# Joining the split of six gated forms, dividing one step of the last down stage, and holding an evacuation behind two weights

## The chip, the cores and the metric

The kernel runs on one core of a Trainium2 chip. The metric is device time in microseconds (us). TensorE is PE in the profile, its weight loads PEld, VectorE is DVE, ScalarE is ACT, GpSimd is POOL, and SP is the engine that issues most of the transfers.

## What is computed

One layer of an encoder on 512 tokens of width 1024: a mixer (a gated short convolution beside a forgetting attention, merged by two sigmoid gates, and an output projection), then a channel mixer, then a norm. The change lies in the channel mixer:

```
h = rms_norm(x, norm_ffn_g[l])
up = causal_dwconv(h @ w_up[l], conv_ffn_w[l])      # 1024 -> 2 * 2816, three taps in time
a, b = jnp.split(up, 2, axis=-1)
x = x + (jax.nn.silu(a) * b) @ w_down[l]            # 2816 -> 1024
```

All data are float32.

## The kernel before, in words

**Numbers in two parts.** Every matmul operand is split: hi is a rounded copy made by ACT (fp32r), lo is the rest, a subtraction on DVE. A product then costs three matmuls: hi·hi, lo·hi, hi·lo. For weights this split is `split()` (L253): ACT's copy at L275 gives `wh_...`, DVE's subtraction at L279 gives `wl_...`. Both have two buffers in turn, so a chunk's split can start when the chunk two places before it is through with PE.

**The stream.** Weights come as a list of chunks (L125 to L154), used in this order by `chunk()` (L290). `split()` also issues loads (L182, on SP) up to seven chunks ahead, as far as raw buffers are free: four for up and P chunks together, four for F chunks.

**The channel mixer.** The 2816 hidden columns are 22 blocks j of 128. `PHASES` (L43) cuts them into j = 0 to 11 and 12 to 21. Each phase has an up stage (one `up(j, ph)` per block, L1141) and then a down stage (`seven(STEPS[ph], ...)`, L824). For each j, `up` makes two products of 48 matmuls (the a half with i = 0, the b half with i = 1) and evacuates each: `mul` on DVE (L1171, times the norm), three taps (`taps`, L564: a scaled copy on ACT at L566, two DVE additions at L567 and L570); after the second, `glu` (L1227) runs the silu on ACT (L1231) and multiplies. In the very last j it also runs a small Sqrt (L1233), so that ACT's table is loaded in time for the last norm. Blocks j of `SUP` are computed by `seven` instead.

**Seven products.** The down products use a seven-product scheme for 2×2 blocks. A pair q holds j = 2q and 2q + 1 (each in two halves of 256 tokens); its seven forms are two blocks of data as they are, and sums. `ge` is the even j, `go` holds the odd j in two pieces and the four sums t1 to t4 (`t13`, L1252, and `t24`, L1256, both on DVE): six forms of 256 columns. `hl` (L1260) splits forms into `gh` (ACT, L1262) and `gl` (DVE, L1263). A step of `STEPS` multiplies one or two (i, q): i is a pair of output blocks. A step is two chunks: P (three products per pair, raw weights) and F (four products, sums of weights that DMAs build in DRAM ahead of time: `make_forms`, L190, with puts on SP at L208 and adds on POOL at L211, a group of up to two steps of the same size). A double step has 18 matmuls in P and 24 in F, a single one 9 and 12. `passes` (L315) runs the hi weights against hi and lo data first, form by form, then the lo weights. P wants the first, second and seventh form of a pair, in that order. In the stream P18/F18 to P29/F29 are the steps of phase 0; P30 to P33 are `SUP` blocks; P34/F34 to P41/F41 are the steps of phase 1.

**Who orders the work.** PE's matmuls and the DMAs are pinned in program order. On ACT, DVE and POOL the framework places an operation when it takes it to be ready, earlier ones of the program first, unless it is told otherwise. The kernel tells it through a list `later` of (first chunk k, cost in us, tags, function). Each `split()` ends with `run_later(k, us)` (L224), which takes from the list what is due and fits an allowance: 1.7 at an up chunk, 1.6 at P, 0.75 at F (4.2, 1.6 and 1.2 while evacuations tagged `e` are waiting in the list). The first due item that doesn't fit ends it. What it runs stands in `after_split()` (L159), so it queues behind the last split's hi on ACT and lo on DVE. `seven` splits one chunk ahead (`split_next`, L818) and calls `flush(wants[name])` (L843), which forces what a P or F chunk needs. `glu` for an odd j first forces the forms of all earlier pairs (L1238), then appends its own, due at chunk k plus 2, 3, 4, or, for the last j of a phase, plus 4, 5, 6; k is the last chunk split so far. In the last j of a phase the multiplication into `go` is itself appended, due at k + 3, on DVE; in others POOL does it at once (L1243).

**The seam.** When the last `up` of a phase has issued its second product, it calls `split_next()` (the first P chunk) and, only if evacuations tagged `e` wait, also flushes them and splits the first F chunk (L1162 to L1166). By then in both phases none wait, so the last evacuation follows P's split at once, and the F chunk is split by `seven`, after P's matmuls in the program.

Of the kernel before, what the change touches and what calls it, by code (L numbers as in the profile page):

```python
# [42 lines left out]
PHASES = ((0, 12), (12, NP))  # L43
# [4 lines left out]
STEPS = (  # L48
    tuple(((i, q), (i, q + 1)) for i, q in ((0, 0), (0, 2), (1, 0), (1, 2), (0, 4), (1, 4)))
    + tuple(((i, q), (i, q + 1)) for i in (3, 2) for q in (0, 2, 4)),  # L50
    (((2, 6), (2, 7)), ((2, 8), (2, 9)), ((0, 6), (0, 7)), ((0, 8), (2, 10)), ((0, 9), (0, 10)))
    + (((1, 6),), ((1, 7), (1, 8)), ((1, 9), (1, 10))),
)

# [16 lines left out]
def block_kernel(ctx, tc, xT, vecs, wv, win, wmix, wo, wup, wst, wdp, outT):  # L71
# [10 lines left out]
    def keep(ins):  # L82
        return tc.keep_in_program_order(ins)
# [72 lines left out]
    later = []  # L156
    held = dict.fromkeys(NRAW, 0)

    def after_split():  # L159

        st = ExitStack()
        for ins in order.values():
            st.enter_context(tc.issue_after(ins))
        return st

    def tag_of(k):
        return "raw" if stream[k][0][0] != "F" else "rf" if k >= ff0 else "rg"

    def load(upto):
        for k in range(len(raws), min(upto, len(stream) - 1) + 1):  # L170
            nm, src, ncol = stream[k]
            tag = tag_of(k)
            if held[tag] == NRAW[tag] or tag not in pools:
                return
            held[tag] += 1
            raw = pools[tag].tile([P, D], F32, tag=tag, name=f"raw_{nm}", bufs=NRAW[tag])
            if k == 0:

                keep(nc.scalar.dma_start(raw[:, VB:ncol], src[:, VB:]))
                keep(nc.sync.dma_start(raw[:, :VB], src[:, :VB]))  # L180
            else:
                keep(nc.sync.dma_start(raw[:, :ncol], src if tag == "raw" else made[src]))  # L182
            raws.append(raw[:, :ncol])
# [34 lines left out]
    def slot():  # L218

        while todo_bg and todo_bg[0][0] <= make_forms.slot:  # L220
            todo_bg.pop(0)[1]()
        make_forms.slot += 1

    def run_later(k, us):  # L224

        n = 0
        while n < len(later):
            if later[n][0] <= k and later[n][1] <= us + 0.1:
                us -= later[n][1]
                with after_split():  # L230
                    later.pop(n)[3]()
            elif later[n][0] <= k:
                return
            else:
                n += 1
# [11 lines left out]
    def flush_only(tags):  # L247

        while n := [n for n, w in enumerate(later) if set(w[2]) & set(tags)]:
            with after_split():  # L250
                later.pop(n[0])[3]()

    def split(hl=None):  # L253

        k = len(parts)
        if k == len(stream):
            return
        nm, _, ncol = stream[k]
        load(k + (LOOK if len(raws) > KB else AHEAD))
        if hl is None:  # L260
            hl = []
            for x in "hl":
                if k == 0:
                    wp.tile([P, PADW[x]], F32, tag=f"pad{x}", name=f"pad_{x}")
                w0 = VOFF if k < KB else 0
                hl.append(wp.tile([P, D], F32R, tag=f"w{x}", name=f"w{x}_{nm}", bufs=2)[:, w0 : w0 + ncol])
        hi, lo = hl
        raw = raws[k]
        if k == 0:
            for cs in (slice(VB, S + H), slice(0, VB)):  # L270
                keep(nc.vector.tensor_copy(hi[:, cs], raw[:, cs]))
        elif k == 1:
            keep(nc.vector.tensor_copy(hi, raw))
        else:
            ins = nc.scalar.activation(hi, raw, AF.Copy)  # L275
            order["hi"] = ins.ins
            if k < KB:
                keep(ins)
        ins = nc.vector.tensor_sub(lo, raw, hi.bitcast(F32))  # L279
        order["lo"] = ins.ins  # L280
        if k < KB:
            keep(ins)
        held[tag_of(k)] -= 1
        parts.append((hi, lo))
        if any(("e",) in w[2] for w in later):
            run_later(k, {"u": 4.2, "P": 1.6, "F": 1.2}[nm[0]])
            return
        run_later(k, {"u": 1.7, "P": 1.6, "F": 0.75, "i": 3.0, "m": 3.0, "d": 0 if nm == "dp1" else 2.1}.get(nm[0], 3.5))
# [163 lines left out]
    for kb in range(KB):  # L452
        x = xs[kb]
# [236 lines left out]
    z, e, o = (ap.tile([n, S], F32, tag="pp", name=nm, bufs=NPP) for nm in ("fz", "fe", "fo"))  # L690
# [83 lines left out]
    for q in (0, 2):  # L774
        f, g = x_sums(slice(q, q + 2))
# [8 lines left out]
    for idx in late:  # L784
        kind, i = divmod(idx, 4)
# [9 lines left out]
    for i in range(n + LA):  # L795
# [8 lines left out]
        if 0 <= i - LA < n:  # L804
            pr, e, qb = units[i - LA]
# [335 lines left out]
    def up(j, ph, rb2, pu=None):  # L1141
        uu = []

        def tap(i, z):
            u = fp.tile([P, S], F32, tag="fu", name=f"fu{j}{i}", bufs=3)
            taps(u, z, CF + 3 * (2 * j + i))
            uu.append(u)

        if j in SUP[ph]:
            c = 2 * SUP[ph].index(j)  # L1150
            slot()
            seven(
                UPD[ph][c : c + 2], NU[ph] + c, {j: USETS[j]}, lambda q, g: up_form(ph, q, g), of="x",
                done=lambda i, banks, ids: merge(ph, j, banks, ids, rb2, tap, uu),
            )
            slot()
            return
        evacs = []
        for i in range(2):
            slot()  # L1160
            p = pu[i] if pu else block(f"up{2 * j + i}", x1h, x1l, True)
            if i and j + 1 == PHASES[ph][1]:  # L1162
                split_next()
                if any(("e",) in w[2] for w in later):
                    flush_only((("e",),))
                    split()  # L1166
            z = [None]

            def mul(i=i, p=p, z=z):
                z[0] = fp.tile([P, S], F32, tag="fz", name=f"fz{j}{i}", bufs=4)  # L1170
                nc.vector.tensor_mul(z[0], p, rb2)  # L1171

            evac = [(0.7, mul), (1.4, lambda i=i, z=z: tap(i, z[0]))]
            if i:
                evac.append((0, lambda: glu(ph, j, uu)))
            if any(("e",) in w[2] for w in later):
                later.extend((0, us, (("e",), acc.last) if x == 0 else (("e",),), f) for x, (us, f) in enumerate(evac))
            else:
                for _, f in evac:
                    f()  # L1180
# [46 lines left out]
    def glu(ph, j, uu):  # L1227
        a, b = uu
        q, k = j // 2, len(parts) - 1
        g0 = place(ph, q)  # L1230
        nc.scalar.activation(a, a, AF.Silu)  # L1231
        if j == NP - 1:
            nc.scalar.activation(tbl, a[: 4 * H, :1], AF.Sqrt, scale=0.0, bias=eps[: 4 * H])  # L1233
        if j % 2 == 0:
            ge = glu.even = fp.tile([P, 2, 2 * P], F32, tag="ge", name=f"ge{q}", bufs=2)
            keep(nc.gpsimd.tensor_mul(ge, a.rearrange(halves_of, h=2), b.rearrange(halves_of, h=2)))  # L1236
            return
        flush_only([("q", x) for x in range(q)])  # L1238
        ge = glu.even
        go = fp.tile([P, 6, 2 * P], F32, tag="gr", name=f"go{q}")  # L1240

        def mul(eng):
            return eng.tensor_mul(go[:, 0:2, :], a.rearrange(halves_of, h=2), b.rearrange(halves_of, h=2))  # L1243

        if j + 1 < PHASES[ph][1]:
            keep(mul(nc.gpsimd))
        else:
            later.append((k + 3, 0.7, (("q", q),), lambda: mul(nc.vector)))
        b11, b12 = ge[:, 0, :], ge[:, 1, :]
        b21, b22, t1, t2, t3, t4 = (go[:, i, :] for i in range(6))  # L1250

        def t13():  # L1252
            nc.vector.tensor_sub(t1, b11, b12)
            nc.vector.tensor_sub(t3, b22, b12)

        def t24():  # L1256
            nc.vector.scalar_tensor_tensor(t2, t1, -1.0, b22, op0=ALU.mult, op1=ALU.subtract)
            nc.vector.scalar_tensor_tensor(t4, t2, -1.0, b21, op0=ALU.mult, op1=ALU.subtract)

        def hl(src, gs):  # L1260
            def f():
                nc.scalar.activation(gh[:, gs, :], src, AF.Copy)  # L1262
                nc.vector.tensor_sub(gl[:, gs, :], src, gh.bitcast(F32)[:, gs, :])  # L1263

            return f


        d = (2, 3, 4) if j + 1 < PHASES[ph][1] else (4, 5, 6)
        w = [(d[0], 0.85, t13), (d[0], 0.85, t24), (d[1], 0.7, hl(ge[:, : 1 + ph, :], slice(g0, g0 + 1 + NF * ph, NF)))]
        w += [(d[x > 0 and 2 or 1], 0.7, hl(go[:, x : x + 2, :], slice(g0 + 1 + x, g0 + 3 + x))) for x in (0, 4, 2)]  # L1270
        at = next((x for x, i in enumerate(later) if ("e",) in i[2]), len(later))
        later[at:at] = [(k + n, us, (("q", q),), f) for n, us, f in w]

# [263 lines left out]
```

## Time and profile before

| what | value |
|---|---|
| median of 3 runs | 694.79 us (694.62 to 695.16) |
| the profiled execution | 694.18 us, span 692.4 us, granted clock 0.997 |
| phase 0's down stage begins (P18) | 465.8 us |
| phase 1's down stage begins (P34) | 631.1 us |
| last matmul ends | 685.8 us |

The profile is one execution. Its rows are instructions, or groups of them: start and duration in us, engine, line, operation, what it writes and reads, shape, count; in brackets the engine's idle time just before it and what ended it. Matmuls overlap: each takes about 0.28 us by its row while the next starts after 0.113, so PE's loss is read from starts. In the list of waits the columns are the total in us, how many, and the longest.

### The profile page before, as it was taken

The numbers are of one execution on the slowest core, as the hardware profiler recorded it, in microseconds if no ns is written. First come the engines' busy times: TensorE is split into PE (matmuls) and PEld (weight loads), VectorE is DVE, ScalarE is ACT, GpSimd is POOL, SyncE is SP. The second block draws the span as 40 slices with busy tenths as digits, with TensorE's granted clock in tenths as the row PEclk, the third lists the DMA queues.
The fourth block names the chain that finished last, engine by engine and source line by source line (L and its number), as shares of the span: only waits on it lengthen the run. The fifth ranks groups of instructions, "written<-read, shape, count | busy, mean of one in ns | idle before, by whom it ended". The sixth has DMA issues, their size and how long they took to land. (4 is left out here: it accounts for less than half of the span.)

```text
span 692.4 us, 14690 instructions
## 1 busy us (share of the span) xinstructions
PE 683.1 (99%) x5936; PEld 680.6 (98%) x5936; DVE 554.2 (80%) x858; ACT 368.3 (53%) x579; POOL 190.5 (28%) x201
## 2 busy tenths in 40 slices
PE   9999999999999999999999999999999999999996
PEld 9999999999999999999999999999999999999995
DVE  6677787877578778769879699998787899988894
ACT  5675755554554444546554555545444544545572
POOL 6134947542020201214400144340100325231000
PEclk9999999999999999999999999999999999999998
DMA  8629999552568586788998498888945996676413
GB/s 308 225 67 293 216 243 204 134 120 92 185 144 221 166 268 205 230 308 213 158 313 241 126 233 222 200 242 231 252 149 167 337 231 157 188 168 182 154 31 122
DMA packets 65012, 137.53 MB, mean 199 GB/s; under 512 B 5760, under 2 KB 30352, under 8 KB 64688
## 3 DMA queue, kind: packets, MB, share of 16 engines
q1 hardware_dynamic: 44664, 107.28, 47.2%
q0 software_dynamic: 18464, 26.03, 23.4%
q10 hardware_dynamic: 1816, 3.29, 1.3%
q8 instruction: 46, 0.75, 0.4%
q14 instruction: 22, 0.18, 0.1%
HBM read 132.31 MB, written 47.71 MB: 260 GB/s over the span
## 5 line engine op out<-in xcount | busy, mean ns | idle before, releaser
L211 POOL DMA_DIRECT2D f<-in_wst_dram x66 | 77.7, 1371 | 27.1 <-DMA f<-f 26.8
L309 PE MATMUL p_up<-x1h,wh_up 128*128 128x256 f32 x416 | 81.2, 276 | 0.0
L309 PE MATMUL p_up<-x1l,wh_up 128*128 128x256 f32 x416 | 81.0, 276 | 0.0
L309 PE MATMUL p_up<-x1h,wl_up 128*128 128x256 f32 x416 | 81.0, 276 | 0.0
L279 DVE TENSOR_TENSOR wl_F<-raw_F,wh_F 128x1024 fp32r<-128x1024 f32 (+1 forms) x42 | 55.9, 1330 | 20.0 <-ACT wh_F L275 20.0
L275 ACT ACTIVATE wh_F<-raw_F 128x1024 fp32r<-128x1024 f32 (+1 forms) x42 | 44.3, 1054 | 39.5 <-PE dn L327 28.7
L309 PEld LDWEIGHTS p_up<-x1h,wh_up 128*128 128x128 f32 x416 | 62.7, 188 | 0.0
L309 PEld LDWEIGHTS p_up<-x1l,wh_up 128*128 128x128 f32 x416 | 62.7, 188 | 0.0
L309 PEld LDWEIGHTS p_up<-x1h,wl_up 128*128 128x128 f32 x416 | 62.6, 188 | 0.0
L309 PE MATMUL p_in<-xgh,wh_in 128*128 128x256 f32 x288 | 56.8, 279 | 0.0
L309 PE MATMUL p_in<-xgh,wl_in 128*128 128x256 f32 x288 | 56.6, 278 | 0.0
L309 PE MATMUL p_in<-xgl,wh_in 128*128 128x256 f32 x288 | 56.5, 278 | 0.0
L279 DVE TENSOR_TENSOR wl_P<-raw_P,wh_P 128x768 fp32r<-128x768 f32 (+1 forms) x42 | 41.7, 992 | 14.7 <-ACT wh_P L275 8.6
L327 PE MATMUL dn<-gh,wh_F 128*128 128x256 f32 x216 | 51.2, 277 | 1.2 <-ACT wh_F L275 1.2
L275 ACT ACTIVATE wh_P<-raw_P 128x768 fp32r<-128x768 f32 (+1 forms) x42 | 35.1, 835 | 32.1 <-PE dn L327 23.2
L327 PE MATMUL dn<-gl,wh_F 128*128 128x256 f32 x216 | 51.0, 276 | 0.0
L1236 POOL TENSOR_TENSOR ge<-fu,fu 128x512 f32<-128x512 f32 x11 | 20.1, 1831 | 110.5 <-DVE fu L570 85.6
L279 DVE TENSOR_TENSOR wl_up<-raw_up,wh_up 128x1024 fp32r<-128x1024 f32 x34 | 43.8, 1288 | 7.4 <-ACT wh_up L275 7.4
L275 ACT ACTIVATE wh_up<-raw_up 128x1024 fp32r<-128x1024 f32 x34 | 35.8, 1054 | 19.4 <-PE p_up L309 9.3
L309 PEld LDWEIGHTS p_in<-xgh,wh_in 128*128 128x128 f32 x288 | 44.7, 188 | 0.7
L309 PEld LDWEIGHTS p_in<-xgl,wh_in 128*128 128x128 f32 x288 | 43.7, 188 | 0.0
L309 PEld LDWEIGHTS p_in<-xgh,wl_in 128*128 128x128 f32 x288 | 43.6, 188 | 0.0
(343 smaller groups left out, 2211.8 us busy)
## 6 DMA issues: line engine op xcount, KB each, us to landing
raw_F<-f SPq DMA_DIRECT2D x41, 512.0 KB, 5.7
raw_up<-in_wup_dram SPq DMA_DIRECT2D x34, 512.0 KB, 5.6
raw_P<-in_wst_dram SPq DMA_DIRECT2D x41, 384.0 KB, 5.4
raw_in<-in_win_dram SPq DMA_DIRECT2D x24, 512.0 KB, 3.6
f<-in_wst_dram POOLq DMA_DIRECT2D x41, 256.0 KB, 6.8
f<-in_wst_dram SPq DMA_DIRECT2D x20, 512.0 KB, 7.1
f<-in_wst_dram POOLq DMA_DIRECT2D x20, 512.0 KB, 9.1
f<-f SPq DMA_DIRECT2D x40, 256.0 KB, 6.5
```

What stands on the lines that cost most here:

```text
L211: return lambda: keep(nc.gpsimd.dma_start(dst, src, accum_op=ALU.add))
L275: ins = nc.scalar.activation(hi, raw, AF.Copy)
L279: ins = nc.vector.tensor_sub(lo, raw, hi.bitcast(F32))
L309: keep(nc.tensor.matmul(out[:, cs], w, x[:, cs], start=start and i == 0 and c == 0, stop=stop and i == 2 and c == len(cut) - 1,))
L327: keep(nc.tensor.matmul(out, wl if x == 1 else wh, xl if x == 2 else xh, start=opens and bk not in seen, stop=closes and bk not in left,))
L1236: keep(nc.gpsimd.tensor_mul(ge, a.rearrange(halves_of, h=2), b.rearrange(halves_of, h=2)))
```

## The change

Three edits. The six forms in `go` are split by one ACT and one DVE operation of 128x1536 in place of three of 128x512 (the cost in the list is 1.7, due at the last of the three times). The step ((0, 8), (2, 10)) of phase 1 becomes two single steps, so the phase has nine, up to P42/F42. And at the end of each phase's up stage the first F chunk is always split, and the last evacuation (mul, taps, glu) stands in `after_split()`.

```
-    (((2, 6), (2, 7)), ((2, 8), (2, 9)), ((0, 6), (0, 7)), ((0, 8), (2, 10)), ((0, 9), (0, 10)))
+    (((2, 6), (2, 7)), ((2, 8), (2, 9)), ((0, 6), (0, 7)), ((0, 8),), ((2, 10),), ((0, 9), (0, 10)))
     + (((1, 6),), ((1, 7), (1, 8)), ((1, 9), (1, 10))),
...
             if i and j + 1 == PHASES[ph][1]:
                 split_next()
-                if any(("e",) in w[2] for w in later):
-                    flush_only((("e",),))
-                    split()
+                split()
+                flush_only((("e",),))
...
             if any(("e",) in w[2] for w in later):
                 later.extend((0, us, (("e",), acc.last) if x == 0 else (("e",),), f) for x, (us, f) in enumerate(evac))
+            elif i and j + 1 == PHASES[ph][1]:
+                with after_split():
+                    for _, f in evac:
+                        f()
             else:
...
         w = [(d[0], 0.85, t13), (d[0], 0.85, t24), (d[1], 0.7, hl(ge[:, : 1 + ph, :], slice(g0, g0 + 1 + NF * ph, NF)))]
-        w += [(d[x > 0 and 2 or 1], 0.7, hl(go[:, x : x + 2, :], slice(g0 + 1 + x, g0 + 3 + x))) for x in (0, 4, 2)]
+        w.append((d[2], 1.7, hl(go, slice(g0 + 1, g0 + 7))))
```

The divided step also makes six groups for `make_forms` in phase 1 where there were five (two of its groups now are one step, or two single ones): three more puts on SP and three more adds on POOL, of the same bytes in all.

## The prediction

> **What bounds the kernel now.** First the page's busy line, then the list of waits for PE alone.
>
> ```profile
> span 692.4 us, 14690 instructions
> PE 683.1 (99%) x5936; PEld 680.6 (98%) x5936; DVE 554.2 (80%) x858; ACT 368.3 (53%) x579; POOL 190.5 (28%) x201
> PE dn L327 <- ACT wh_F L275: 1.2, 2, 0.7
> PE dn L327 <- DVE wl_F L279: 0.4, 1, 0.4
> PE p_up L327 <- DVE wl_up L279: 0.2, 1, 0.2
> ```
>
> PE is busy for 99% of the span, and the diff leaves its matmuls as they are: a product of a step costs three matmuls whether steps are joined or not. So only holes in PE's stream count. DVE's and ACT's time matters where a weight or a form is late for PE, and nowhere else. The profiled execution took 694.18 us, 1.77 over its span and 0.61 under the median 694.79. I make the sum as a difference and put it on the median. A difference of 0.2%, 1.39 us, is about what a measurement of this kernel can tell from no change.
>
> Where are the holes? The timeline of PE, at the two F chunks that open the down stages:
>
> ```profile
> 468.62 0.38 PE L327 MATMUL dn<-gh,wh_F 128*128 128x256 f32 x1 [0.66 <-ACT wh_F L275]
> 468.84 0.29 PE L327 MATMUL dn<-gl,wh_F 128*128 128x256 f32 x1
> ...
> 633.78 0.38 PE L327 MATMUL dn<-gh,wh_F 128*128 128x256 f32 x1 [0.50 <-ACT wh_F L275]
> 634.00 0.29 PE L327 MATMUL dn<-gl,wh_F 128*128 128x256 f32 x1
> ```
>
> An undisturbed matmul starts 0.113 us after the one before it (a fence of Part 3: nine of them from 655.67 to 656.69). At F18 and F34 the start is missed, and the second start is 0.22 behind instead of 0.11, so a hole costs its idle time, 0.17 of a matmul's tail that idleness does not count, and 0.11 of restart: 0.93 us at F18, 0.77 us at F34. All that the change can aim at is these 1.70 us, 0.24% of the time. The other two waits of the list lie in the up stages, at weights that the hold does not touch.
>
> Why is wh_F late? ACT's timeline around the two places:
>
> ```profile
> 466.99 0.63 ACT L1231 ACTIVATE fu<-fu 128x512 f32<-128x512 f32 x1 [0.89 <-DVE fu L570]
> 467.53 1.04 ACT L275 ACTIVATE wh_F<-raw_F 128x1024 fp32r<-128x1024 f32 x1
> 468.80 0.73 ACT L566 ACTIVATE fu<-fz,vec 128x512 f32<-128x512 f32 x1 [0.23 <-DVE fz L1171]
> 469.43 0.83 ACT L275 ACTIVATE wh_P<-raw_P 128x768 fp32r<-128x768 f32 x1
> ...
> 631.19 1.28 ACT L1233 ACT_TABLE_LOAD   x1
> 632.49 0.29 ACT L1233 ACTIVATE tbl<-fu,ex 32x1 f32<-32x1 f32 x1
> 632.69 1.04 ACT L275 ACTIVATE wh_F<-raw_F 128x1024 fp32r<-128x1024 f32 x1
> ```
>
> At F18 ACT waits 0.89 us for a tap of DVE to run the silu, at F34 it runs the silu and a table load of 1.28, and the split of the F chunk stands behind both. Its buffer had been free since the last block ended: P18's and P34's 18 matmuls (2.03) lie between that and the hole, so it ended at 468.62 − 0.82 − 2.03 = 465.77, and at 631.08.
>
> **Part 1: the hold.** Now F18 and F34 are split before the last evacuation. How soon a split follows its buffer's last use, a chunk of the stage shows:
>
> ```profile
> 650.91 0.28 PE L327 MATMUL dn<-gh,wh_P 128*128 128x256 f32 x1
> ...
> 652.47 0.53 ACT L275 ACTIVATE wh_P<-raw_P 128x384 fp32r<-128x384 f32 x1 [0.94 <-PE dn L327]
> ```
>
> The chunk begun at 650.91 is through with its 12 wh matmuls at 652.27; the split that takes its buffer starts 0.2 later. So F18's split starts 0.2 after the block's end and takes 1.04, done at 1.25, while P18 and P34 keep PE for 2.03. DVE's part (1.2 us, done at 2.5) is needed 16 matmuls later, at 3.8. Both holes go: −0.93 and −0.77.
>
> What is late next? Behind the held weights on DVE stand mul, the two taps and, through glu's own flush, the forms of the pair before. At F18 this matters. Before, P18's split ran one of q = 4's three form splits and glu the rest, early, while DVE would otherwise have idled:
>
> ```profile
> 464.44 1.66 ACT L1262 ACTIVATE gh<-go 128x512 fp32r<-128x512 f32 x3
> ...
> 466.82 1.28 DVE L1263 TENSOR_TENSOR gl<-go,gh 128x512 fp32r<-128x512 f32 x2
> 468.02 0.68 DVE L1171 TENSOR_TENSOR fz<-p_up,rb_n 128x512 f32<-128x512 f32 x1
> 468.63 1.21 DVE L279 TENSOR_TENSOR wl_F<-raw_F,wh_F 128x1024 fp32r<-128x1024 f32 x1
> 469.76 0.74 DVE L567 SCALAR_TENSOR_TENSOR fu<-fz,vec,fu 128x511 f32<-128x511 f32 x1
> 470.42 0.95 DVE L279 TENSOR_TENSOR wl_P<-raw_P,wh_P 128x768 fp32r<-128x768 f32 x1
> ```
>
> Now the joined split costs 1.7, F18's allowance is 0.75, so it waits for glu's flush and stands behind F18's split on both engines. Counted from the block's end: ACT wh_F to 1.2, silu to 1.85, joined form 1.5 to 3.35, tap 0.72 to 4.1, then wh_P of P19 0.85 to 4.9; P19 starts at 42 × 0.113 = 4.74. DVE wl_F to 2.5, mul to 3.15, joined form (after ACT's 3.35) to 5.1, tap 0.74 to 5.8, wl_P of P19 to 6.75; PE wants it 12 matmuls into P19, at 6.1 to 6.25. So P19 loses about 0.2 + 0.5; with one restart I take **+0.75**. Below it is 0 (P19's split goes ahead of tap and form), above it 1.4 (both taps go ahead of it). At P35 no form is left to flush, so nothing of this kind; ACT's table load just moves behind F34's split, and P35's 0.83 fits before 4.74: 0.
>
> **Part 2: one form split for three.** The three back-to-back splits take ACT 1.66 and DVE 1.89 from the first start to the last end (fences here and below). No row has 1536 elements; I go by the two nearest sizes:
>
> ```profile
> L275 ACT ACTIVATE wh_up<-raw_up 128x1024 fp32r<-128x1024 f32 x34 | 35.8, 1054 | 19.4 <-PE p_up L309 9.3 <-PE dn L327 5.1 <-issue 3.8
> L1263 DVE TENSOR_TENSOR gl<-go,gh 128x512 fp32r<-128x512 f32 x33 | 22.3, 697 | 0.0
> L1262 ACT ACTIVATE gh<-go 128x512 fp32r<-128x512 f32 x33 | 19.2, 618 | 3.5 <-DVE go L1257 2.0 <-POOL go L1243 1.1 <-DVE go L1258 0.5
> ```
>
> ACT: 1054 + (1054 − 618) = 1.49 us. DVE: wl_F's 1.21 + (1.21 − 0.68) = 1.74, with the 0.68 of one form from the next fence. So each of the 11 sets saves ACT 0.17 and DVE 0.15. [...] None of this is PE's time. What it costs is overlap: ACT and DVE no longer work on different thirds at once, and the first forms wanted come only with the last. In the up stages of both phases the sets have a slack of several chunks, with one doubtful place, the block of the third wait in the list, whose wl_up is late already because form splits stand ahead of it (its 0.2 idle, tail and restart make 0.43):
>
> ```profile
> 604.84 0.42 DVE L1258 SCALAR_TENSOR_TENSOR go<-go 128x256 f32<-128x256 f32 x1
> 605.17 0.68 DVE L1263 TENSOR_TENSOR gl<-go,gh 128x512 fp32r<-128x512 f32 x1
> 605.77 0.68 DVE L1171 TENSOR_TENSOR fz<-p_up,rb_n 128x512 f32<-128x512 f32 x1
> 606.37 1.80 DVE L1263 TENSOR_TENSOR gl<-go,gh 128x512 fp32r<-128x512 f32 x2
> 608.09 0.74 DVE L567 SCALAR_TENSOR_TENSOR fu<-fz,vec,fu 128x511 f32<-128x511 f32 x1
> 608.75 1.21 DVE L279 TENSOR_TENSOR wl_up<-raw_up,wh_up 128x1024 fp32r<-128x1024 f32 x1
> ```
>
> The joined form can start on ACT only at 605.26, when the last of t1 to t4 is there, and on DVE at 606.8, to 608.5; the tap and wl_up follow, 0 to 0.5 us later than now, or wl_up slips ahead and the hole closes. I take +0.2, from −0.43 to +1.0.
>
> **Part 3: the last set and the divided step.** Here the sum turns. The last set's dues count from k, the last chunk split when glu runs. The hold makes k one greater: mul is due at k + 3, the t's at k + 4, the even form at k + 5, the six forms at k + 6. In phase 0, k is F18, and k + 6 is F21; F chunks allow 0.75, the joined split asks 1.7, so it goes to P22, the first to want q = 5. P22's own split waits until P21's 12 wh matmuls are done: 12 × 0.113 + 0.2 = 1.56 after P21's start. Then wh_P to 2.4, the form on ACT to 3.9, on DVE to 5.7; P22 starts at 4.74, and asks for q = 5's gl after 9 matmuls, at 5.76. Just in time: +0.1 (0 to 0.3).
>
> In phase 1, k is F34, k + 6 is F37, and again the set goes to the next P chunk, P38. That is now ((2, 10),), the first to want q = 10, and both its forerunner and itself are single. How fast single chunks go, before's single step (P39, F39) shows:
>
> ```profile
> 655.67 0.28 PE L327 MATMUL dn<-gh,wh_P 128*128 128x256 f32 x1
> ...
> 656.69 0.28 PE L327 MATMUL dn<-gh,wh_F 128*128 128x256 f32 x1
> ...
> 658.13 0.38 PE L327 MATMUL dn<-gh,wh_P 128*128 128x256 f32 x1
> ```
>
> From P37's start: its 6 wh matmuls free the buffer at 0.68 + 0.2 = 0.88; wh_P 0.53 to 1.41; form on ACT 1.49 to 2.9; form on DVE 1.74 to 4.7, and 0.05 until PE starts. P38 starts at 21 × 0.113 = 2.37 and asks for gh of the second form after 2 matmuls, for its gl after 3, at 2.71. PE stands from 2.71 to 4.75 at most: 2.04, and 0.11 of restart: **+2.15**. Before, the same set had this room:
>
> ```profile
> 643.70 1.66 ACT L1262 ACTIVATE gh<-go 128x512 fp32r<-128x512 f32 x3
> ...
> 646.15 0.28 PE L327 MATMUL dn<-gh,wh_P 128*128 128x256 f32 x1
> ...
> 644.70 1.89 DVE L1263 TENSOR_TENSOR gl<-go,gh 128x512 fp32r<-128x512 f32 x3
> ```
>
> It was done at 646.59, and P37, begun at 646.15, got to q = 10 after 6 matmuls, at 646.83. What hid it was the whole F36 (24 matmuls, 2.7 us) between its split and its use; between P38's split and its use lie only F37's 12. Bounds: 1.5, if DVE and ACT were quicker by their back-to-back overlap and single starts slower; 2.4 with two restarts. The price of dividing beside this: one more P and F split and three more DMAs each for SP and POOL, of the same bytes; the halves hide beside PE as P39's do: 0, up to +0.5 if a raw load queues behind an f<-f on SP.
>
> **Sum:** −0.93 − 0.77 + 0.75 + 0.2 + 0.1 + 2.15 = **+1.5 us**, on 694.79: **696.3 us**. With all low bounds (−1.7 + 0 − 0.43 + 0 + 1.5) it is 694.2, with all high ones (−1.7 + 1.4 + 1.0 + 0.3 + 2.4 + 0.5) 698.7.
>
> **Rivals.** (a) P19 and the block with the late wl_up cost nothing, the wait at P38 stays smaller than worked out: −1.7 + 1.5 to 2.15, about 694.8. For it: one order of ACT and DVE suffices, and before's order often puts a split between two taps. Chance 0.17.
> (b) The other side, faster: the six forms get done ahead of P38's split, because they need only DVE's t's and the order is the framework's as well as the planner's. Then P38 does not wait, −1.7 to −0.6 remains, 693.4. It decides at one point: whether L1262's joined operation starts before P37 does. Against it: the planner queues it behind P38's wh on ACT and wl on DVE. Chance 0.12.
> (c) The hold misses: another operation of ACT or DVE slips ahead of F18 and F34, both holes stay, and the rest is paid: 696.3 + 1.7 = 698.0. Chance 0.04.
> (d) The clock falls after the hole at P38: 3.4 us at half speed would add 1.7, 698.0. The hole of 0.66 at F18 left the granted clock at 1.00:
>
> ```profile
> 466.00:478.00 12.00, 11.35 (x100) 11.15 (x99) 11.54 (x18) 6.64 (x10) 0.00 (x0) 1.00 0.96 247
> ```
>
> [...] Chance 0.05.
>
> **How the numbers follow.** The forecast has 0.62, 695.4 to 697.6; its lower third lies within 0.2%. Slower: 0.42 of it, with (c) and (d) 0.51. Same: 0.20 of it, with most of (a) 0.36. Faster: (b) and the rest of (a), 0.13. The range 694.0 to 698.2 takes in the bounds and leaves out (b) and the far end of (c) and (d).
>
> **What would show it.** Right: no PE hole at F18 and F34; PE's longest wait some 2 us at P38, for DVE's gl of L1266 or so, at about 648; a hole of 0.3 to 1 us near 471 at P19. Wrong: the joined form starting well before P37's end, or holes in the up stages that before has not.

## The result, and the profile after

The median is 697.36 us against 694.88 us for the kernel before (six executions each, before from 694.62 to 695.16). One of the six executions of after, 1157.65 us at a mean granted clock of 0.557, is left out of the ratio and of every comparison below; the other five lie between 696.77 and 697.8, with a median of 697.18. The ratio is 1.0028 [1.0017, 1.0039], so the change made the kernel slower, by some 0.3%. The forecast was 696.3, its range 694.0 to 698.2. The profiled execution took 696.77 us with a span of 695.0, so the difference to explain is 695.0 − 692.4 = 2.6 us.

The profile page of after, its first and its busy line, and then the list of waits for PE alone (total in us, how many, the longest):

```profile
span 695.0 us, 14677 instructions
PE 683.3 (98%) x5936; PEld 680.5 (98%) x5936; DVE 552.8 (80%) x838; ACT 367.0 (53%) x559; POOL 195.6 (28%) x204
```

```profile
PE p_up L327 <- DVE wl_up L279: 2.0, 2, 1.6
PE dn L327 <- DVE gl L1266: 1.4, 1, 1.4
...
PE dn L327 <- DVE wl_F L279: 0.4, 1, 0.4
```

PE's busy time is 683.3 against 683.1. DVE and ACT were spared 1.4 and 1.3 us of busy time, and the kernel became slower all the same. Before's longest line, `wh_F` with 1.2 in two waits, is gone. Two new waits stand in its place: one for `gl` and one of 1.6 for `wl_up`. (The second `wl_up` wait, and the 0.4 for `wl_F`, are waits that before has too. The list of after also has a wait of 0.2 at L477, in the mixer.) Here they are on PE's timeline of after:

```profile
445.00 0.28 PE L327 MATMUL p_up<-x1l,wh_up 128*128 128x256 f32 x1
446.83 0.62 PE L327 MATMUL p_up<-x1h,wl_up 128*128 128x256 f32 x3 [1.55 <-DVE wl_up L279]
...
610.86 0.28 PE L327 MATMUL p_up<-x1l,wh_up 128*128 128x256 f32 x1
611.57 0.51 PE L327 MATMUL p_up<-x1h,wl_up 128*128 128x256 f32 x2 [0.43 <-DVE wl_up L279]
...
649.33 0.28 PE L327 MATMUL dn<-gl,wh_P 128*128 128x256 f32 x1
649.67 0.38 PE L327 MATMUL dn<-gh,wh_P 128*128 128x256 f32 x1
651.47 0.38 PE L327 MATMUL dn<-gl,wh_P 128*128 128x256 f32 x1 [1.41 <-DVE gl L1266]
651.69 0.28 PE L327 MATMUL dn<-gh,wh_P 128*128 128x256 f32 x1
```

A hole is read from starts: the distance to the matmul before, less the 0.113 of an undisturbed start, and 0.11 more where the second matmul comes 0.22 behind. At P38 that is 0.23 (649.67) + 1.69 (651.47) + 0.11 = **2.03 us**. In the block that runs at 444 us, the first product of j = 10 in phase 0 (called up20 here), it is 1.72 + 0.11, and its first matmul was already 0.15 + 0.11 late for `wh_up`, a wait too short for a bracket: **2.10 us** together. The block at 611.57 has 0.60 + 0.11 = 0.71, where before's had 0.43: **+0.28**. F18, F34 and P19 have no hole. The small one of before at 658.13, where the prediction's fence has a row of 0.38 (0.20 by starts), is gone. The sum of differences, −0.93 − 0.77 − 0.20 + 2.03 + 2.10 + 0.28 = +2.51 us, accounts for the span's 2.6.

The hole at P38 is the one that was forecast. The operations behind it, on the timelines of ACT and DVE of after:

```profile
648.14 1.48 ACT L1265 ACTIVATE gh<-go 128x1536 fp32r<-128x1536 f32 x1
...
649.65 1.76 DVE L1266 TENSOR_TENSOR gl<-go,gh 128x1536 fp32r<-128x1536 f32 x1 [0.82 <-ACT gh L1265]
```

The joined form starts on ACT right behind the split of P38's weights, and DVE starts when ACT ends. PE wants the form at 649.4 and gets its `gl` at 651.4. The two engines work on the set one after the other, 1.48 and then 1.76 us, and PE has nothing to do meanwhile.

The hole in up20 was not forecast. DVE's timeline of after:

```profile
438.85 0.41 DVE L1256 TENSOR_TENSOR go<-ge 128x256 f32<-128x256 f32 x1
...
442.11 1.20 DVE L1266 TENSOR_TENSOR gl<-ge,gh 128x256 fp32r<-128x256 f32 x1
443.24 1.75 DVE L1266 TENSOR_TENSOR gl<-go,gh 128x1536 fp32r<-128x1536 f32 x1
444.90 0.74 DVE L567 SCALAR_TENSOR_TENSOR fu<-fz,vec,fu 128x511 f32<-128x511 f32 x1
445.56 1.21 DVE L279 TENSOR_TENSOR wl_up<-raw_up,wh_up 128x1024 fp32r<-128x1024 f32 x1
```

and of before, around the same block:

```profile
442.64 2.00 DVE L279 TENSOR_TENSOR wl_up<-raw_up,wh_up 128x1024 fp32r<-128x1024 f32 x1
444.57 0.41 DVE L1253 TENSOR_TENSOR go<-ge 128x256 f32<-128x256 f32 x1
```

In before, up20's `wl_up` is made at 442.64, and the pair's t1 to t4 begin only after it. In after the t's begin 5.7 us earlier, the whole set of pair q = 3 is finished ahead of up20's weights, and `wl_up` starts 2.9 us later. So a whole set has changed places with a weight. Why it does that is the main question for the experiments.

### The profile page after: what moved, and what is told of

The parts are those of the page before. It is cut to its first block, busy times and chain, and to the rows that moved or that the text cites. A ratio compares the mean times of both kernels' runs of the same rounds, so it can differ in the third digit from the quotient of the medians.

```text
span 695.0 us, 14677 instructions
## 1 busy us (share of the span) xinstructions
PE 683.3 (98%) x5936; PEld 680.5 (98%) x5936; DVE 552.8 (80%) x838; ACT 367.0 (53%) x559; POOL 195.6 (28%) x204
## 4 chain that ended last, share of the span: by engine, by line
PE 86%; DVE 9%; ACT 1%; issue 1%; DMA 1%; POOL 0%; SPq 0%; DVEq 0%; POOLq 0%; ACTq 0%
PE dn L327 27%; PE p_in L309 14%; PE p_up L309 14%; PE p_wo L309 6%; PE p_up L327 4%; PE yc L309 3%; PE ya L309 3%; DVE wl_up L279 2%; DVE fu L567 2%; PE p_q L309 2%; PE p_k L309 2%; PE o L658 2%; PE pa L477 2%; PE pb L479 1%; PE tp L641 1%; DVE gl L1266 1%
## 5 line engine op out<-in xcount | busy, mean ns | idle before, releaser
L211 POOL DMA_DIRECT2D f<-in_wst_dram x69 | 79.8, 1364 | 29.7 <-DMA f<-f 23.8
```

The lines of the kernel that those rows point to most:

```text
L211: return lambda: keep(nc.gpsimd.dma_start(dst, src, accum_op=ALU.add))
```

## The experiments

**The theories.** Theory A: the list `later` did it. The three form splits asked 3 × 0.7 = 2.1 us of allowance, and the first of them came due one chunk before the other two; the joined one asks 1.7, all of it at the last due. The evacuations of this stage stand in the same list, so they drain sooner, `glu` of the odd j comes sooner (two chunks, worked out by hand from the list), and its line "force the forms of all earlier pairs" then catches a set that was not yet due. Rival theory B: the form of the instruction did it, since one operation of 1.75 can't be interleaved with a weight. For the hole at P38 the same two stand against each other, and a third theory H, that the hold alone delays the last set enough. All ratios are to the kernel before on the same chip; its medians there were 695.04, 695.16 and 695.26.

**One edit alone: the joined split.** Before, with this only:

```
-        w += [(d[x > 0 and 2 or 1], 0.7, hl(go[:, x : x + 2, :], slice(g0 + 1 + x, g0 + 3 + x))) for x in (0, 4, 2)]
+        w.append((d[2], 1.7, hl(go, slice(g0 + 1, g0 + 7))))
```

> Before with the joined split of six forms alone. Theory (the list of due work moves): the joined item is cheaper in the list, so the queue of evacuations empties earlier, glu(9) comes two chunks earlier and forces q = 3's whole set ahead of up20's weights: the hole of some 2.1 us in block up20 is here as in the changed kernel, F18's and F34's holes (0.93 and 0.77) stay, P37 waits 0 to 0.2: 697.0 us, 2.1 over before. Rival (the hold makes the hole in the up stage, by moving what the framework places there): no hole at up20, 694.9.

Measured: 696.93 us, 1.0027 [1.0015, 1.0039]. On PE's timeline of this kernel the hole in up20 is there, in the same size:

```profile
445.56 0.28 PE L327 MATMUL p_up<-x1l,wh_up 128*128 128x256 f32 x1
447.40 0.62 PE L327 MATMUL p_up<-x1h,wl_up 128*128 128x256 f32 x3 [1.56 <-DVE wl_up L279]
```

So the hole belongs to the join, not to the hold or the divided step. The two holes that the hold aims at did not stay as before: F18's was gone, F34's had grown. The list of waits shows one `wh_F` wait, where before has two of 0.7 and less:

```profile
PE dn L327 <- ACT wh_F L275: 1.2, 1, 1.2
```

With starts, that hole is 1.45 against 0.77; why it grew is not shown here. At F18 pair q = 4's set had been made earlier, by the same shift of the list.

**One edit alone: the hold.** Before, with the seam of the change:

```
                 split_next()
-                if any(("e",) in w[2] for w in later):
-                    flush_only((("e",),))
-                    split()
+                split()
+                flush_only((("e",),))
...
+            elif i and j + 1 == PHASES[ph][1]:
+                with after_split():
+                    for _, f in evac:
+                        f()
```

> Before with the hold alone: three splits, double step ((0,8),(2,10)). Theory: F18's and F34's holes go (-1.7), the up stages are as before, the last set comes one chunk later but its thirds overlap, so P37 and P22 wait 0 to 0.4 and P19 0 to 0.5: 693.2 to 694.1. Rival (the late last set costs PE about 2 us whatever its form): a hole of 1.5 to 2 at P37, 694.7 to 695.2.

Measured: 695.20 us, 1.0005 [0.9996, 1.0014]: both holes are gone and nothing is won. The gain is spent at P37. PE's and DVE's timelines of this kernel:

```profile
645.87 0.38 PE L327 MATMUL dn<-gh,wh_P 128*128 128x256 f32 x1
647.62 0.38 PE L327 MATMUL dn<-gl,wh_P 128*128 128x256 f32 x1 [1.36 <-DVE gl L1266]
```

```profile
644.53 1.29 DVE L1266 TENSOR_TENSOR gl<-go,gh 128x512 fp32r<-128x512 f32 x2
645.74 1.22 DVE L279 TENSOR_TENSOR wl_F<-raw_F,wh_F 128x1024 fp32r<-128x1024 f32 x1
646.88 0.69 DVE L1266 TENSOR_TENSOR gl<-go,gh 128x512 fp32r<-128x512 f32 x1
```

Two thirds of the last set are in time, the last third stands behind F37's `wl_F`. The hole is about 1.75 us (1.75 between the starts, less 0.11, and 0.11 of restart). My expectation of 0 to 0.4 fell here: theory H holds for this kernel, and the set is late even as three operations, because the hold moves all its dues one chunk back.

**The list's timing kept, the joined operation taken apart.** After, with one item in the list that runs three splits of 128x512 in a row:

```
-        w.append((d[2], 1.7, hl(go, slice(g0 + 1, g0 + 7))))
+        three = [hl(go[:, x : x + 2, :], slice(g0 + 1 + x, g0 + 3 + x)) for x in (0, 4, 2)]
+        w.append((d[2], 1.7, lambda: run_all(three)))
```

> The changed kernel, its one list item now running three pairs of 128x512 in before's order: every due time and order of the list is the changed kernel's, only the operation is split again. Theory (list, not operation, makes the hole at up20; operation, not list, makes the size of the one at P38): the hole at up20 stays at 1.5 to 2.5, the one at P38 falls from 2.0 to about 0.5: 1.5 under the changed kernel. Rival (the long operation makes both): both fall under 0.6, 3 under the changed kernel, 1 under before.

Measured: 696.11 us, 1.0020 [1.0008, 1.0033]. PE's timeline:

```profile
444.70 0.28 PE L327 MATMUL p_up<-x1l,wh_up 128*128 128x256 f32 x1
447.52 0.74 PE L327 MATMUL p_up<-x1h,wl_up 128*128 128x256 f32 x4 [2.54 <-DVE wl_up L279]
```

The hole in up20 is not only there with three small operations, it is larger: 2.82 between the starts, less 0.11, and 0.11 of restart, 2.82 us. Theory B falls for up20. At P38 the hole shrinks from 2.03 to about 0.48 by starts, and no line of the list of waits names it any more. So P38's hole is made by the size of the operation, up20's by what stands in the list, its price and its due, which are both after's here.

**The last set earlier.** After, with all that belongs to the last set of a phase due one chunk earlier:

```
-        d = (2, 3, 4) if j + 1 < PHASES[ph][1] else (4, 5, 6)
+        d = (2, 3, 4) if j + 1 < PHASES[ph][1] else (3, 4, 5)
...
-            later.append((k + 3, 0.7, (("q", q),), lambda: mul(nc.vector)))
+            later.append((k + 2, 0.7, (("q", q),), lambda: mul(nc.vector)))
```

> The changed kernel with the last set of a phase due one chunk earlier (mul k + 2; t's, even form, six forms k + 3, 4, 5), which makes the joined split fall on P21 and P37. Theory: the hole at P38 (2.0) goes, since P37's split stands a whole F36 ahead; the one at up20 (2.1) stays: 2.0 under the changed kernel, about level with before (694.9). Rival (P38's hole comes from the single steps being too short for their own weights): it stays, time as the changed kernel.

Measured: 694.88 us, 0.9999 [0.9990, 1.0007]. The joined subtraction now starts four microseconds sooner, and P38 has no wait; up20 keeps its 1.6. DVE's timeline and the list of waits of this kernel:

```profile
645.65 1.76 DVE L1266 TENSOR_TENSOR gl<-go,gh 128x1536 fp32r<-128x1536 f32 x1 [0.39 <-ACT gh L1265]
```

```profile
PE p_up L327 <- DVE wl_up L279: 2.0, 2, 1.6
```

The two new holes are independent of each other: this kernel is 2.3 us faster than after by the medians (697.18 − 694.88) and 1.9 by the profiled spans (695.0 − 693.1), and only P38's hole of 2.03 was taken away.

**The hold with the last set earlier, no join, no divided step.** Before, with the two edits just shown, the seam and the earlier dues:

```
+                split()
+                flush_only((("e",),))
...
-        d = (2, 3, 4) if j + 1 < PHASES[ph][1] else (4, 5, 6)
+        d = (2, 3, 4) if j + 1 < PHASES[ph][1] else (3, 4, 5)
```

> Before with the hold, and the last set of a phase due one chunk earlier (mul k + 2, rest k + 3, 4, 5), so that it falls on the chunks of before; no joining, no divided step. Theory (the hold is worth its two holes once the last set isn't late): no hole at F18, F34, P37, none new in the up stages: 1.7 under before, 693.3. Rival (the hold pushes some other split behind, as the hold alone did at P37, with 1.74): a hole of 1 to 2 at P37 or P38 stays, 694.5 to 695.2.

Measured: 693.72 us, 0.9977 [0.9967, 0.9986]. No hole at F18, F34, P37 or in up20. Beside the hold alone this is 1.5 us less, near the 1.75 of P37's hole. So the hold is worth its gain, once it doesn't drag the last set back.

**One edit alone: the divided step.** Before, with this only:

```
-    ((0, 6), (0, 7)), ((0, 8), (2, 10)), ((0, 9), (0, 10))
+    ((0, 6), (0, 7)), ((0, 8),), ((2, 10),), ((0, 9), (0, 10))
```

> Before with the divided step alone. Theory (dividing is nearly free and useless by itself: q = 10's set is done at P37 anyway): holes at F18 and F34 as before, none new, 0 to 0.3 over before. Rival (one more P and F split and three more DMAs on SP and POOL make weights late): a new hole near P38 or P39 of 0.5 or more.

Measured: 694.51 us, 0.9991 [0.9982, 1.0000]: a little faster or the same. F18 and F34 keep their holes (0.94 and 0.80), no new one comes, and the small one at 658.13 is gone. The additional loads, puts and adds cost nothing that shows.

**The joined operation with the list's timing of before.** After with the earlier last set (the experiment with that name; the expectation calls it a4), and the join's item cut in an empty one and the real one, so that the list counts 2.1 as before, 0.7 of it due one chunk before the rest:

```
-        w.append((d[2], 1.7, hl(go, slice(g0 + 1, g0 + 7))))
+        six = hl(go, slice(g0 + 1, g0 + 7))
+        w += [(d[1], 0.7, lambda: None), (d[2], 1.4, six)] if j + 1 < PHASES[ph][1] else [(d[2], 1.7, six)]
```

> The changed kernel with the last set earlier (as in a4), and in the list, except for the last set, an empty item of 0.7 beside a joined item of 1.4, so that the list adds up to before's 2.1 at before's due times, while the operation stays joined. Theory (the list's sum makes the hole at up20): glu(9) comes at up21 again, the hole of 2.1 there goes; q = 4's joined split falls behind F18's, as the prediction had it, and P19 waits 0 to 0.9 by the prediction's working; 692.3 to 693.7 in all. Rival (a joined operation cannot be placed well among taps and weights, whatever the list says): a hole of over 1 us stays in the up stage of phase 0, 694 or more.

Measured: 693.31 us, 0.9975 [0.9965, 0.9985]. This is the reverse of the experiment with three operations: the same joined operation, the old price at the old dues, and up20's hole is gone. With that, theory A is shown from both sides.

Which of the two in the list counts, price or due, neither experiment tells, since both times the two changed together. The order of the list can be followed by its rules. At up18's split the allowance is 4.2. In before a third of q = 2's set (0.7) is due there and is counted; `glu` forces the other two thirds, and what is forced is not counted; then a tap of 1.4 no longer fits. In after nothing of the joined item is due yet, `glu` forces all of it uncounted, and the tap fits. By that one tap the list is ahead, and glu(9) runs at up19 instead of up21. So here the due decides, not the price: three items of 1.7 in all at before's dues leave glu(9) at up21, three of 2.1 in all at the last due bring it to up19. These two orders are worked out from the list; no run times them.

In place of up20's hole one comes at P19. PE's and DVE's timelines:

```profile
472.41 0.86 PE L327 MATMUL dn<-gh,wl_P 128*128 128x256 f32 x5 [0.30 <-DVE wl_P L279]
```

```profile
467.17 1.23 DVE L279 TENSOR_TENSOR wl_F<-raw_F,wh_F 128x1024 fp32r<-128x1024 f32 x1 [0.60 <-ACT wh_F L275]
468.31 0.68 DVE L1170 TENSOR_TENSOR fz<-p_up,rb_n 128x512 f32<-128x512 f32 x1
469.06 1.76 DVE L1266 TENSOR_TENSOR gl<-go,gh 128x1536 fp32r<-128x1536 f32 x1
470.74 0.75 DVE L567 SCALAR_TENSOR_TENSOR fu<-fz,vec,fu 128x511 f32<-128x511 f32 x1
471.40 0.95 DVE L279 TENSOR_TENSOR wl_P<-raw_P,wh_P 128x768 fp32r<-128x768 f32 x1
```

This is the order that the prediction worked out for after (weight, mul, joined form, tap, weight), in the kernel in which its premise is true; the hole is 0.58 us by starts.

**The change without its join.** After with the three splits of before; hold and divided step stay:

```
-        w.append((d[2], 1.7, hl(go, slice(g0 + 1, g0 + 7))))
+        w += [(d[x > 0 and 2 or 1], 0.7, hl(go[:, x : x + 2, :], slice(g0 + 1 + x, g0 + 3 + x))) for x in (0, 4, 2)]
```

> The changed kernel with the three separate splits again: hold and divided step alone. Theory (the join costs the hole at up20 and three quarters of the one at P38): up20 as before, no hole; P38 waits about 0.5, since its first third is ready 0.6 after wh and the next thirds overlap; F18, F34 gone: 693.7 to 694.3, 0.6 to 1.2 under before. Rival (the late last set is what costs, as in the hold alone with 1.74 at P37): 1.5 to 2 at P38, 695.

Measured: 692.68 us, 0.9965 [0.9952, 0.9978]. Neither new hole is there, and F18, F34 and P38 have none; the time is 1 us under the expected range, which had put 0.5 at P38. DVE's timeline around P38:

```profile
645.81 0.68 DVE L1266 TENSOR_TENSOR gl<-go,gh 128x512 fp32r<-128x512 f32 x1
646.41 0.55 DVE L279 TENSOR_TENSOR wl_P<-raw_P,wh_P 128x384 fp32r<-128x384 f32 x1
646.91 1.29 DVE L1266 TENSOR_TENSOR gl<-go,gh 128x512 fp32r<-128x512 f32 x2
```

A third goes ahead of P38's weight and two thirds behind it, all done by 648.2. Compare the hold alone, where the last third had no divided step in front of it and stood behind a whole F chunk. So the two other edits fit each other, and one edit turned them into a loss: the join costs about 4.5 us by the medians (697.18 − 692.68), 4.0 by the profiled spans (695.0 − 691.0), and its two holes are 4.13.

**Without the join, all the rest, and with the join where it is safe.** First the hold, the divided step and the earlier last set with three splits; second the same, but with the last set of each phase joined (after those sets no set follows whose place in the list could shift):

```
+        if j + 1 < PHASES[ph][1]:
+            w += [(d[x > 0 and 2 or 1], 0.7, hl(go[:, x : x + 2, :], slice(g0 + 1 + x, g0 + 3 + x))) for x in (0, 4, 2)]
+        else:
+            w.append((d[2], 1.7, hl(go, slice(g0 + 1, g0 + 7))))
```

> Hold, divided step, three splits, and the last set one chunk earlier. Theory (the divided step already gives the three splits enough room, so the earlier due adds nothing): holes as in the kernel without the join, 692.4 to 693.0, 0.35% under before. Rival (there is still something of the last set on PE's path): another 0.3 or more under that, 692.3 or less.

> As the one before, with the last set of each phase joined, every other set in three. Theory (joined, due a whole F chunk ahead of its use, a set costs PE nothing, and gains nothing, as DVE's and ACT's time there hides): no hole at P38 or P22, within 0.3 of the one before. Rival (ACT and DVE free sooner helps the chunks behind): 0.3 or more faster.

Measured: 693.23 us, 0.9966 [0.9952, 0.9980], and 692.36 us, 0.9955 [0.9943, 0.9968]. The second beats both kernels and is the fastest of the study, 0.9 us under the first where 0.3 at most was expected, but its interval overlaps that of the first and that of the change without its join. The lists of waits for PE show where the first lost, first kernel:

```profile
PE pa L477 <- ACT xgh L458: 1.1, 1, 1.1
...
PE p_up L327 <- DVE wl_up L279: 0.4, 1, 0.4
```

second kernel:

```profile
PE pa L477 <- DVE wh_v L273: 0.2, 1, 0.2
PE p_up L327 <- DVE wl_up L279: 0.2, 1, 0.2
```

Most of the difference lies at L477, in the mixer, which none of these edits touch, so I don't put it down to the join. With the divided step, the earlier dues bring nothing that can be told from none (0.9966 beside 0.9965).

## Why the prediction was right, and where it failed

The sign held, and the size came out higher: +1.5 was forecast, +2.3 by the medians (697.18 − 694.88) and +2.6 by the profiled spans came. The terms, in the order of the prediction:

- **F18 −0.93 and F34 −0.77: right.** ACT's timeline of after shows both F chunks split ahead of the silu and of the table load:

```profile
468.35 1.07 ACT L275 ACTIVATE wh_F<-raw_F 128x1024 fp32r<-128x1024 f32 x1 [2.81 <-PE p_up L309]
469.32 0.61 ACT L1234 ACTIVATE fu<-fu 128x512 f32<-128x512 f32 x1
...
632.80 1.07 ACT L275 ACTIVATE wh_F<-raw_F 128x1024 fp32r<-128x1024 f32 x1 [2.27 <-PE p_up L309]
633.77 0.62 ACT L1234 ACTIVATE fu<-fu 128x512 f32<-128x512 f32 x1
...
635.14 1.28 ACT L1236 ACT_TABLE_LOAD   x1
```

  The hold alone takes both away. At F18 it is not the only thing that does: the join alone did it too.
- **P38 +2.15: right, 2.03 measured.** The joined operations took 1.48 and 1.76, against 1.49 and 1.74 taken from the two nearest sizes. The mechanism is shown by three operations in place of one (0.48) and by the earlier dues (none). Only, the hold has a part of its own in it: alone, with the step not divided, it makes a hole of 1.75 at P37. The prediction said that the whole F36 hid the set there, and kept to before's dues in saying so.
- **P19 +0.75: wrong here, 0 measured.** The step that failed is "it waits for glu's flush and stands behind F18's split": in after q = 4's set was done long before. DVE's timeline of after has it at

```profile
462.42 1.75 DVE L1266 TENSOR_TENSOR gl<-go,gh 128x1536 fp32r<-128x1536 f32 x1
```

  Where the list keeps before's timing, the set does stand there, and the hole is 0.58, in the `wl_P` part that was put at 0.5.
- **P22 +0.1: 0 measured**, within its bounds.
- **The block with the late `wl_up`, +0.2: +0.28 measured**, within its bounds. What sets its size stays open: it is 0.43 or 0.44 in before, with the divided step alone and in the fastest kernel, about 0.7 in most others, with the join and without it, and none with three operations in one item, so the joined form is not its cause.
- **"In the up stages of both phases the sets have a slack of several chunks": this step failed, and it is worth 2.10 us.** I looked at what the join does to ACT and DVE in a chunk, and found it to be nothing. But the item in the list is also the clock by which the list runs. With the joined item at the last due, 0.7 less is counted one chunk earlier, what stands behind runs sooner, `glu` too, and the rule that it forces older sets turns a slack set into an urgent one ahead of a weight. By the prediction's own test ("wrong: holes in the up stages that before has not") it was wrong there.

The two errors, 0.75 that did not come and 2.10 that was not forecast, have the same cause, the shifted list, and partly cancel. That the total came within 1 us or so is therefore in part luck: the mechanisms at F18, F34 and P38 were foreseen, the largest single loss was not. Of the rivals, (a) named P19 rightly but not the new hole, (b) fell since the joined form started at 648.14, behind P38's weights, (c) fell since both holes went, and (d) did not occur: the clock after both holes of after stayed at 1.00 (the last part). Its 3.4 us at half speed came in another kernel, the one with three operations in one item, behind a hole of 2.54 us, and cost some 1.4 us there.

## What to carry to other kernels

In a hand-written order, an item's cost and due are not only an estimate of its time but the clock of all that stands behind it: whoever joins items must follow the list to the end of the stage, or keep the old costs and dues and test that alone. One large operation in place of three saved its engines little here (0.18 us on ACT, 1.66 to 1.48, and 0.14 on DVE, 1.89 to 1.75) and took away the overlap of the two engines in a chain and every gap between them in which a weight could go; at P38, where the consumer waits for the first third, that was the dearer side (a hole of 2.03 us, and of 0.48 with three operations). A hold that removes a wait should be tried together with the dues that are counted from it, since here it was worth nothing alone and 1.4 us with the last set one chunk earlier.

## What the runs showed of the hardware

After one short hole PE was slower. In the kernel with three operations in one item, PE stood for 2.54 us, and then its clock fell. PE's timeline shows pairs of matmuls 0.43 us apart from 448.62 on, where 0.23 is usual; the windows of that kernel (length, then busy time and count for PE, PEld, DVE, ACT and POOL, the granted clock, and DMA) show it too:

```profile
448.62 0.63 PE L309 MATMUL p_up<-x1l,wh_up 128*128 128x256 f32 x2
449.05 0.63 PE L309 MATMUL p_up<-x1h,wh_up 128*128 128x256 f32 x2
```

```profile
447.50:448.50 1.00, 0.98 (x8) 0.98 (x9) 1.00 (x2) 0.34 (x1) 0.00 (x0) 0.98 0.05 9
448.50:452.00 3.50, 3.50 (x19) 3.50 (x19) 2.35 (x4) 0.38 (x1) 1.00 (x1) 0.52 0.94 306
452.00:460.00 8.00, 8.00 (x73) 8.00 (x72) 5.33 (x9) 3.18 (x5) 2.36 (x3) 1.00 0.96 239
```

The granted clock is 0.52 over 3.5 us: 19 matmuls in place of 31, some 1.4 us lost at 0.113 a matmul. The pairs' 0.43 for 0.23 put the clock at about half; at half, the 0.98 and 0.52 of the first two windows make some 3.4 us of it, an estimate (0.04 before 448.50 and 3.36 after). It came one microsecond after the hole ended (447.52), not in it. Of the twelve executions of this kernel three have a mean clock of 0.994 and take 697.0 to 697.6 (the profiled one is among them); seven, at 0.996 or 0.997, take 695.4 to 696.2; the other two, 697.88 and 699.6 at 0.996, the clock does not explain. So the clock may have fallen in three of the twelve; of the executions without a profile that is not shown. Behind after's own holes, with 1.55 and 1.41 idle, the windows of after show no fall:

```profile
446.80:450.30 3.50, 3.47 (x30) 3.47 (x31) 2.39 (x4) 2.20 (x3) 0.00 (x0) 1.00 0.68 186
...
651.50:655.00 3.50, 3.50 (x30) 3.50 (x31) 2.50 (x4) 2.18 (x3) 0.00 (x0) 1.00 0.59 211
```

Behind the last matmul the clock falls to half in before and in after. The clock's records in these two traces have it in full for 682.666 us in before, up to 687.59, and for 686.079 us in after, up to 690.34: 200 and 201 times 3.413 us, the difference between the two. So in these two traces the clock fell on a step of 3.413 us, with 1.79 us of idle in the step before in before (PE's last row ends at 685.80) and 1.96 in after (688.38). After's two holes put 1.56 and 1.48 us of idle into one such step each, without a fall. What decides whether the clock falls no run here shows.
